# A ring of raw expert weights that keeps its 12 slots to the end, and overflow tables that borrow one of them

## The chip, the core and the metric

The kernel runs on one core of a Trainium2 chip. The metric is the device time of one execution in microseconds (us). The engines that count here are TensorE (PE, matmuls and transposes), VectorE (DVE), ScalarE (ACT), GpSimd (POOL, which also starts the gathers and scatters) and SyncE (SP, which starts the weight loads). Each runs its own list of instructions in order and waits on semaphores for the others.

## The reference

One layer of a hybrid encoder for 1024 tokens of width 1024, in float32. An input projection feeds differential attention and a state-space recurrence; their outputs are projected, added and normalized to h. Then comes the part that the change touches, a mixture of 32 experts: each token goes to the best two experts of the best one of four groups.

```python
for i in range(DEPTH):
    proj = x @ w_in[i]
    ...
    mix = jnp.concatenate([a_out, s_out], axis=-1) @ w_out[i]
    h = _layernorm(alpha * x + mix, ln1_g[i], ln1_b[i])
    moe = _hier_moe(h.reshape(b_ * s_, d_), ...)
    x = _layernorm(alpha * h + moe, ln2_g[i], ln2_b[i])

def block_fn(args):          # 128 rows of one expert
    tok, w, e = args
    xb = h2d[tok]
    hid = jax.nn.silu(xb @ w_gate[e]) * (xb @ w_up[e])
    yb = hid @ w_down[e]
    return yb * w[:, None].astype(yb.dtype)
```

w_gate and w_up are 1024 x 512 per expert, w_down 512 x 1024. An expert that gets more than 128 rows needs further blocks.

## The kernel before

The stages up to the router run until about 590 us and are not touched. Behind them each of the 32 experts is computed for one block of 128 rows. Its weights, 6 MB, come as six chunks of 1 MB: g0 and g1 (the two halves of the gate), u0 and u1 (up), d0 and d1 (down). The chunks are used in the order g0 u0 g1 u1 of expert e, then d0 d1 of expert e - 1; chunk number n counts along that list, so chunk 63 is d1 of expert 9, in short 9d1.

Each chunk passes through two rings. SyncE loads it into a slot of the raw ring (tile rw, `load_next`, loads at L1166 and L1170). Then `split_next` makes two halves of its bits, wh and wl, in one of three places of a second ring: ScalarE casts to wh (L169), VectorE subtracts to get wl (L150). TensorE multiplies both (`product`, L1223 for y, L1232 for g and u): 12 matmuls of 128x512 per chunk, three for each of the four row blocks, 72 per expert.

Around the weights, per expert: GpSimd gathers its 128 rows of h into gx; `tokens` turns them on TensorE into xT (8 transposes, L1196), ScalarE casts xT to xe and VectorE subtracts for the low half; `hidden` takes the activation of g on ScalarE (gx, L1202), multiplies by u on VectorE (L153), turns it on TensorE (hT, 4 transposes, L1206) and splits it into he; `result` scales y on ScalarE (yo, L1239), adds the residual on VectorE (L159), and GpSimd scatters yo to DRAM. xT and y lie in two pairs of PSUM banks: y(e), then xT(e+4), then y(e+2) share one pair.

The raw ring has 12 slots up to chunk 62 (`deep`, NRAW). From chunk NDEEP = 63 on only 6 of them are used (NLESS), and at the product of chunk 75 the other 6 are given back. One of these takes the tables that say which experts have further blocks (`overflow_blocks`, an Area named over), another the constants of the last LayerNorm (lnc, L1331 and L1332).

The order in which the program names the operations is not the order on the engines: a scheduler places each engine's list by its own estimate of durations and by what each instruction has to wait for. So a changed wait can move instructions on every engine. A loop for further blocks follows the experts; with these inputs it runs zero times.

Of the kernel before, what the change touches and what calls it, by code (L numbers as in the profile page):

```python
# [11 lines left out]
F32 = mybir.dt.float32  # L12
F32R = mybir.dt.float32r
BF16 = mybir.dt.bfloat16
# [31 lines left out]
ORDER = (4, 5, 6, 7, 0, 1, 2, 3)    # the tiles of tokens as attention finishes them  # L46
# [3 lines left out]
class Slots:  # L50
    """Eight-KiB pieces of each partition, handed out by the time since they were given back."""
# [29 lines left out]
class Area:  # L81
    """Tiles by name, cut from a few slots; a name that comes again gets the same place."""

    def __init__(self, sl, n, name):
        self.sl, self.tiles = sl, [sl.get([P, 2048], F32, f"{name}{j}") for j in range(n)]
        self.used, self.at, self.turn = [0] * n, {}, {}
# [18 lines left out]
    def close(self):  # L105
        self.sl.put(*self.tiles)
# [3 lines left out]
def tile_kernel(ctx: ExitStack, tc: tile.TileContext, I: dict, out: bass.AP, dbg=None):  # L110
# [15 lines left out]
    def bank(name, which=0):  # L126
        """512 columns: two banks in turn for which = 0, two others for which = 1, or one of these for 2 or 3."""
        if which == 1:
            turn[0] ^= 1
            which = 2 + turn[0]  # L130
        return psum.tile([P, 512], F32, tag=f"bank{which}", name=name, bufs=1 if which else 2)
# [35 lines left out]
    def split(hi, lo, raw, eng=V):  # L167
        """raw = hi + lo, exactly up to twice the bits of a float32r significand."""
        S.copy(hi, raw)  # L169
        sub(lo, raw, hi.bitcast(F32), eng)  # L170
# [12 lines left out]
    def load_w(ct):  # L183
        """A column tile of w_in."""
        r = misc.get("wr", [KT, P])
        SP.dma_start(r, w_in[:, ct * P:(ct + 1) * P].rearrange("(k p) n -> p k n", p=P))
        wraw[ct] = r
# [28 lines left out]
    def proj(ct):  # L216
        """128 columns of x @ w_in, with columns on the partitions: [128, 1024 tokens] in PSUM."""
        first = ct == 12
        if first:
            turn_x(0)  # L220
        wt = split_w(ct)
        o = bank2(f"proj{ct}")

        def products(kt, halves):
            h_, l_ = xh[kt // 2][:, kt % 2, :], xl[kt // 2][:, kt % 2, :]
            for n, (w_, x_) in enumerate(((0, h_), (0, l_), (1, h_))):
                for hs in halves:
                    PE.matmul(o[:, hs], wt[kt // 4][:, w_, kt % 4, :], x_[:, hs],  # L228
                              start=(kt == 0 and n == 0), stop=(kt == KT - 1 and n == 2))

        for halves in ((HALVES[0:1], HALVES[1:2]) if first else (HALVES,)):
            if first and halves == HALVES[1:2]:
                turn_x(1)
                sl.put(*xraw)
            for kt in range(KT):
                products(kt, halves)
        return o

    def proj_u(c4):
        """128 channels of u, laid out as [(7 - step, channel), group, block of 8 steps]."""  # L240
# [37 lines left out]
    def vexp(x, n, name):  # L278
# [19 lines left out]
        # The power of two in two factors, so that each is a normal number.  # L298
# [71 lines left out]
    # a_re and a_im with states on the partitions, twice over.  # L370
# [33 lines left out]
    # Powers 0..8 of lam_bar.  # L404
# [19 lines left out]
    # (lam_bar - 1) / lam  # L424
# [17 lines left out]
    # Unit phases of 8 steps to the powers 1, 2, .., 64; the sine's sign turns in the lower half.  # L442
# [50 lines left out]
    # cos and sin of the phase of block 16 j + l: of l, and of 16 j.  # L493
# [30 lines left out]
    # The working tiles in slots by the order of their last uses.  # L524
# [13 lines left out]
    def ssm_prepare(u):  # L538
        """The matrices of four groups: into the state, within a block of 8 steps, and out of it; and the phases."""
# [16 lines left out]
        # Kernels of lag 0..7, and the Toeplitz matrix over a block's steps.  # L556
# [26 lines left out]
        # Phases of the blocks' starts.  # L583
# [6 lines left out]
    def ssm_unit(u, UT, z2, made):  # L590
        """The recurrence over blocks of 8 steps, y and gelu(y) of four groups."""
        uo = 4 * (u % 2)
        Wm, Tm, M, C, Sn = made
        # What each block adds to the state, turned back by the block's phase.
# [25 lines left out]
        # Twice gelu(y) = y (1 + tanh(sqrt(2/pi) (y + 0.044715 y^3)))  # L620
# [41 lines left out]
    def proj_v(h):  # L662
        """A head's values, with tokens on the partitions."""
# [15 lines left out]
    def proj_k(h):  # L679
        """Per head and part, the rows [high; low] of k."""  # L680
# [37 lines left out]
    def glu(ct, half):  # L718
# [8 lines left out]
        # The sigmoid of a number is a half and half the hyperbolic tangent of its half.  # L727
# [25 lines left out]
    def queries(h):  # L753
        """A head's queries, high and low parts, each on both halves of the partitions."""
# [43 lines left out]
    def weigh(h, i, p_, L, RL, j, po):  # L798
        """p0 / l0 - lam p1 / l1 but for a factor l0, transposed, times the values."""
# [17 lines left out]
    def normalize(h, g, po, RL):  # L817
        """RMS norm over a head's channels, for the four tiles of tokens 4 g .. 4 g + 3."""
# [31 lines left out]
    # Two heads at a time: at first a large tile of one with a small one of the other, then from the last tile down.  # L850
# [63 lines left out]
    def layernorm(t_, w_, o_, gb, quick=False):  # L914
        """o_ = LayerNorm(t_) gb[0] + gb[1], by way of w_. By half rows on one engine where nothing else runs."""
# [31 lines left out]
    iof = cp.tile([P, P], F32, name="iof")      # 0..127 along the row  # L947
    G.iota(iof, pattern=[[1, P]], base=0, channel_multiplier=0, allow_small_or_imprecise_dtypes=True)
    iom = rtile("iom", [NE])                    # 0..31, less 64
    ts(iom, iof[:, 0:NE], 64.0, ALU.subtract)  # L950
    # Of each token's two choices: token - 4096, token + 1024 k - 4096, weight.
# [6 lines left out]
    tri = rtile("tri", [P], BF16)               # 1 where the row is before the column  # L958
# [4 lines left out]
    # LR and LI have had their last readers.  # L963
    flat = [a_.rearrange("p k g -> p (k g)").bitcast(BF16) for a_ in (LR, LI)]
    O = flat[0][:, 0:2 * NT * NE].rearrange("p (k t e) -> p k t e", k=2, t=NT)                 # the chosen experts as rows of 0 and 1
# [3 lines left out]
    rk = cp.tile([P, 2, NT], F32, name="rk")    # rank among the rows of the chosen expert  # L969
    # Of each place in an expert's first block: the token and the row of its result, less 4096 if any, and the weight.  # L970
# [4 lines left out]
    first = cp.tile([P, NE], F32, name="first")     # ALPHA where it is the token's first choice  # L975

    def route(i0, n, eng):
        ti = slice(i0, i0 + n)

        def first_max(v, w, name):  # L980
            """The maximum along the last axis, and its first place as 0 and 1."""
# [35 lines left out]
        # Rows that an expert gets from earlier tokens.  # L1017
# [5 lines left out]
        # The two probabilities, renormalised: 1 / (1 + e) and e / (1 + e), e = exp(second - first).  # L1023
# [80 lines left out]
    w_g, w_u, w_d = I["w_exp_gate"][0], I["w_exp_up"][0], I["w_exp_down"][0]  # L1104
    NRAW, NSPL, NXG = 12, 3, 5
    NDEEP, NLESS = 63, 6
    # The slots of what is needed last hold the chunks after those split first, until these are split.
# [12 lines left out]
    def deep(n):  # L1120
        """The slot of a chunk, and how many chunks may be loaded and not yet split with it."""
        if NSPL <= n < NSPL + NLENT:
            return lent[n - NSPL], NRAW + NLENT
        if n < NDEEP:
            return raw_ring[(n if n < NSPL else n - NLENT) % NRAW], NRAW + (NLENT if n < NRAW + NSPL + NLENT else 0)
        return raw_ring[n % NLESS], NLESS
# [23 lines left out]
    def rows(a, kt):  # L1150
        """The columns of a that meet rows kt % 4 + 4 p of the kt // 4th 512 rows of a weight."""
        return a[:, 512 * (kt // 4) + kt % 4:512 * (kt // 4) + 512:4]
# [4 lines left out]
    def load_next():  # L1157
        n = st_["load"]
        e, m = order[n]
# [31 lines left out]
    def tokens(e):  # L1191
        """The rows of an expert's block, transposed and split."""
# [52 lines left out]
    # Blocks past the first of each expert: how many, whose, and each row's block and place.  # L1245
    def overflow_blocks():
        op = Area(sl, 1, "over")
# [39 lines left out]
        # Those of a first block get block -1.  # L1287
# [10 lines left out]
    for n, (e, m) in enumerate(order):  # L1298
# [19 lines left out]
        if n == NDEEP + NRAW:  # L1318
            spare = raw_ring[NLESS:]
            sl.back(spare)  # L1320
            meta, place, blk = overflow_blocks()
# [6 lines left out]
    sl.back(raw_ring[:NLESS])  # L1328
    # What the last LayerNorm needs besides the experts' results.
# [89 lines left out]
    def moments(i):  # L1419
        """Less the mean, and the variance plus epsilon, of a tile's rows."""  # L1420
# [58 lines left out]
```

## Time and profile before

| | us |
|---|---|
| median of 3 runs | 1226.17 |
| lowest and highest | 1224.1, 1226.75 |
| span of the profiled execution | 1226.3 |
| TensorE busy in it | 1093.3 (89%) |
| VectorE busy | 970.5 (79%) |
| ScalarE busy | 701.1 (57%) |

The profile is of one execution; its span runs from the first to the last instruction and lies within the spread of the three runs, so sums can be made on it. Busy times of an engine are means over stages; the expert stage is read in stretches of its own. A row of a timeline gives the start, the duration and what the instruction writes and reads; buffer numbers are left out, so rw9d stands for both 9d0 and 9d1. In brackets stands the idle time before the instruction and what ended it.

### The profile page before, as it was taken

Reading aid. Unit: us, or ns where it says so; the run is one execution under the profiler, and the core shown is the slowest. Engines: PE = TensorE matmul, PEld = TensorE weight load, DVE = VectorE, ACT = ScalarE, POOL = GpSimd, SP = SyncE. Lnnn points to the kernel's source line nnn. Section 1 sums busy time; section 2 is a strip of 40 time slices with the busy share of each in tenths; the row PEclk is TensorE's granted clock in tenths of the full one; section 3 lists DMA queues with packets and bytes.
Section 4 is the critical chain, followed back from the end, with each engine's and each line's share of the span. In section 5 each row is a group of like instructions: output and inputs, shape, how many; then the busy total and the mean of one; then the engine's idle time right before and its main releaser. Section 6 shows DMA issues by size and latency. Waiting matters only on the chain. (4 is left out here: it accounts for less than half of the span.)

```text
span 1226.3 us, 15046 instructions
## 1 busy us (share of the span) xinstructions
PE 1093.3 (89%) x5313; PEld 902.2 (74%) x5313; DVE 970.5 (79%) x1409; ACT 701.1 (57%) x941; POOL 390.7 (32%) x279
## 2 busy tenths in 40 slices
PE   7987998889899999976999999999999999999910
PEld 6876787767688788875888887877787787777700
DVE  5598678556877664466999998899999989999857
ACT  3222333445675642233788886777778777877702
POOL 0058465322443442343125640213212212121034
PEclk9988999997899899976999999999999999999955
DMA  5641111211201463563899994999999999999666
GB/s 195 148 93 48 42 56 28 57 34 35 68 2 35 141 234 111 208 238 117 312 350 393 374 380 164 358 322 373 361 373 335 366 366 342 394 345 370 239 236 192
DMA packets 89213, 271.01 MB, mean 221 GB/s; under 512 B 30128, under 2 KB 50608, under 8 KB 64688
## 3 DMA queue, kind: packets, MB, share of 16 engines
q1 hardware_dynamic: 65968, 245.18, 54.6%
q0 software_dynamic: 11216, 23.61, 6.6%
q10 hardware_dynamic: 11952, 1.23, 0.7%
q8 instruction: 43, 0.70, 0.2%
q14 instruction: 34, 0.28, 0.1%
HBM read 254.12 MB, written 27.26 MB: 229 GB/s over the span
## 5 line engine op out<-in xcount | busy, mean ns | idle before, releaser
L1138 POOL DMA_INDIRECT moe_dram<-yo,idx x32 | 65.4, 2042 | 337.5 <-DVE yo L159 330.6
L1133 POOL DMA_INDIRECT gx<-h_dram,idx x32 | 82.3, 2570 | 127.9 <-PE g L1232 51.3
L228 PE MATMUL proj<-xh,wa 128*128 128x512 f32 x256 | 76.5, 406 | 1.6 <-ACT ssm L669 1.6
L228 PE MATMUL proj<-xh,wb 128*128 128x512 f32 x256 | 76.0, 409 | 1.6 <-ACT ssm L669 1.6
L1066 PE MATMUL mix<-woh,mx 128*128 128x512 f32 x256 | 73.7, 398 | 0.0
L781 ACT ACTIVATE p<-s,nm 128x1024 f32<-128x1024 f32 (+7 forms) x64 | 47.2, 743 | 26.3 <-DVE nm L794 19.7
L228 PEld LDWEIGHTS proj<-xh,wb 128*128 128x128 f32 x256 | 50.0, 198 | 12.2 <-ACT ssm L669 1.8
L228 PEld LDWEIGHTS proj<-xh,wa 128*128 128x128 f32 x256 | 49.0, 195 | 11.4 <-ACT ssm L669 1.8
L1239 ACT ACTIVATE yo<-y,WT 128x1024 f32<-128x1024 f32 (+1 forms) x33 | 35.9, 1092 | 36.4 <-PE y L1223 36.3
L169 ACT CAST xe<-xT 128x1024 fp32r<-128x1024 f32 x32 | 32.5, 1014 | 40.9 <-PE xT L1196 32.5
L1066 PEld LDWEIGHTS mix<-woh,mx 128*128 128x128 f32 x256 | 47.5, 190 | 9.4 <-DVE mx L150 0.3
L776 PE MATMUL s<-kk,qh 128*128 128x512 f32 (+3 forms) x96 | 42.2, 439 | 11.3 <-ACT p L781 10.4
L159 DVE SCALAR_TENSOR_TENSOR yo<-gx,first,yo 128x1024 f32<-128x1024 f32 (+1 forms) x33 | 41.1, 1249 | 10.3 <-ACT yo L1239 10.1
L1196 PE MATMUL xT<-ident,gx 128*128 128x128 f32 x256 | 37.7, 291 | 9.8 <-DMA gx<-h_dram,idx 9.8
L1196 PEld LDWEIGHTS xT<-ident,gx 128*128 128x128 f32 x256 | 36.9, 207 | 12.6 <-DMA gx<-h_dram,idx 10.4
L150 DVE TENSOR_TENSOR xe<-xT,xe 128x1024 fp32r<-128x1024 f32 x32 | 39.0, 1219 | 8.0 <-ACT xe L169 7.5
L794 DVE TENSOR_REDUCE nm<-s 128x1 f32<-128x1024 f32 (+3 forms) x32 | 32.6, 1020 | 14.6 <-PE s L778 14.6
L814 PE MATMUL po<-vv,half 128*128 128x128 f32 x288 | 42.9, 290 | 0.0
L228 PE MATMUL proj<-xl,wa 128*128 128x512 f32 x128 | 42.8, 404 | 0.0
L228 PE MATMUL proj<-xl,wb 128*128 128x512 f32 x128 | 42.6, 407 | 0.0
L1202 ACT ACTIVATE gx<-g 128x512 f32<-128x512 f32 x32 | 19.1, 596 | 40.3 <-PE g L1232 40.3
L1066 PE MATMUL mix<-wol,mx 128*128 128x512 f32 x128 | 42.1, 397 | 0.0
(862 smaller groups left out, 3547.7 us busy)
## 6 DMA issues: line engine op xcount, KB each, us to landing
misc<-in_w_in_dram SPq DMA_DIRECT2D x16, 512.0 KB, 4.5
mo<-moe_dram SPq DMA_DIRECT2D x11, 512.0 KB, 6.4
xr<-in_x_dram SPq DMA_DIRECT2D x8, 512.0 KB, 5.8
wo_raw<-in_w_out_dram SPq DMA_DIRECT2D x4, 1024.0 KB
xa<-in_x_dram SPq DMA_DIRECT2D x8, 512.0 KB, 4.4
h_dram<-xa SPq DMA_DIRECT2D x8, 512.0 KB, 4.5
out_dram<-mo SPq DMA_DIRECT2D x8, 512.0 KB, 5.9
mo<-moe_dram POOLq DMA_DIRECT2D x5, 512.0 KB, 13.2
```

Source lines behind the costliest of these rows:

```text
L150: eng.tensor_tensor(out=out_, in0=a, in1=b, op=ALU.subtract)
L159: return V.scalar_tensor_tensor(out=out_, in0=a, scalar=s, in1=b, op0=op0, op1=op1)
L228: PE.matmul(o[:, hs], wt[kt // 4][:, w_, kt % 4, :], x_[:, hs], start=(kt == 0 and n == 0), stop=(kt == KT - 1 and n == 2))
L776: PE.matmul(s_[:, c0:c0 + w], qd[0][:, c, tk], kk[h][:, c, c0:c0 + w], start=True, stop=False)
L781: S.activation(p_[:, c, 0:n], s_[:, 0:n], AF.Exp, bias=nm[:, c:c + 1], accum_out=L[:, j, c:c + 1])
L794: V.tensor_reduce(out=nm[:, c:c + 1], in_=s_[:, 0:n], axis=AX.X, op=ALU.max, negate=True)
L814: PE.matmul(po[:, j * P:(j + 1) * P], aT[:, k, :], vv[k // 4][:, k % 4, h * P:(h + 1) * P], start=(k == 0), stop=(k == i))
L1066: PE.matmul(o[-(hs.start > 0)][:, hs], mx[:, m_, kt, :], (woh, wol)[w_][kt // 2][:, kt % 2, hs], start=(kt == 0 and n == 0), stop=(kt == K ...
L1133: G.indirect_dma_start(out=dst, out_offset=None, in_=h_dram[:, :], in_offset=bass.IndirectOffsetOnAxis(ap=ix, axis=0), bounds_check=T - 1, ...
L1138: G.indirect_dma_start(out=moe_dram[:, :], out_offset=bass.IndirectOffsetOnAxis(ap=ix, axis=0), in_=src, in_offset=None, bounds_check=2 * ...
L1196: PE.transpose(b_[:, kt * P:(kt + 1) * P], rows(g_, kt), ident)
L1239: S.mul(yo[:, hs], y[:, hs], WT[:, e:e + 1])
```

## The change

The ring keeps 12 slots for all chunks. The overflow tables are made when chunk 63 (9d1) is about to be loaded, in the slot of the ring that 9d1 then takes; the earlier user of that slot is chunk 51, d1 of expert 7. The load of 9d1 therefore waits for the last operation on the tables. The constants of the last LayerNorm are loaded behind the last weights, when the 12 slots are given back. Comments are removed, which moves lines by 2 or 3 (L1166 becomes L1169, L1202 becomes L1205, L1239 becomes L1242).

```diff
 class Area:
-    def __init__(self, sl, n, name):
-        self.sl, self.tiles = sl, [sl.get([P, 2048], F32, f"{name}{j}") for j in range(n)]
+    def __init__(self, sl, n, name, key=None):
+        self.sl, self.key = sl, key
+        self.tiles = [sl.get([P, 2048], F32, f"{name}{j}") if key is None else sl.at(key, [P, 2048], F32, name)
+                      for j in range(n)]
...
     def close(self):
-        self.sl.put(*self.tiles)
+        if self.key is None:
+            self.sl.put(*self.tiles)
...
-    NDEEP, NLESS = 63, 6
+    NOVER = 63
...
     def deep(n):
         if NSPL <= n < NSPL + NLENT:
             return lent[n - NSPL], NRAW + NLENT
-        if n < NDEEP:
-            return raw_ring[(n if n < NSPL else n - NLENT) % NRAW], NRAW + (NLENT if n < NRAW + NSPL + NLENT else 0)
-        return raw_ring[n % NLESS], NLESS
+        return raw_ring[(n if n < NSPL else n - NLENT) % NRAW], NRAW + (NLENT if n < NRAW + NSPL + NLENT else 0)
...
     def load_next():
         n = st_["load"]
+        if n == NOVER:
+            over.extend(overflow_blocks(deep(n)[0]))
...
-    def overflow_blocks():
-        op = Area(sl, 1, "over")
+    over = []
+    def overflow_blocks(key):
+        op = Area(sl, 1, "over", key)
...
         product(e, m)
-        if n == NDEEP + NRAW:
-            spare = raw_ring[NLESS:]
-            sl.back(spare)
-            meta, place, blk = overflow_blocks()
...
-    sl.back(raw_ring[:NLESS])
+    meta, place, blk = over
+    sl.back([deep(n)[0] for n in range(len(order) - NRAW, len(order))])
     lnc = sl.get([P, 2, D], F32, "lnc")
     SP.dma_start(lnc[:, 0, :], I["ln2_g"][0].partition_broadcast(P))
     SP.dma_start(lnc[:, 1, :], I["ln2_b"][0].partition_broadcast(P))
```

The loads around 9d1 on SyncE before (rw9d1_... is the raw tile of 9d1, and so on):

```order
L1170 DMA rw11g1_5912<-in_w_exp_gate_dram 128x2048
L1170 DMA rw11u1_5933<-in_w_exp_up_dram 128x2048
L1166 DMA rw10d0_5964<-in_w_exp_down_dram 128x2048
L1166 DMA rw9d1_5842<-in_w_exp_down_dram 128x2048
L1170 DMA rw11g0_5863<-in_w_exp_gate_dram 128x2048
L1170 DMA rw11u0_5891<-in_w_exp_up_dram 128x2048
L1331 DMA lnc_9248<-in_ln2_g_dram 128x1024
L1332 DMA lnc_9248<-in_ln2_b_dram 128x1024
L1166 DMA rw10d1_5993<-in_w_exp_down_dram 128x2048
L1170 DMA rw12g0_6014<-in_w_exp_gate_dram 128x2048
```

The same place afterwards:

```order
L1173 DMA rw12g0_5906<-in_w_exp_gate_dram 128x2048
L1173 DMA rw12u0_5934<-in_w_exp_up_dram 128x2048
L1173 DMA rw12g1_5955<-in_w_exp_gate_dram 128x2048
L1173 DMA rw12u1_5976<-in_w_exp_up_dram 128x2048
L1169 DMA rw11d0_6007<-in_w_exp_down_dram 128x2048
L1173 DMA rw13g0_6057<-in_w_exp_gate_dram 128x2048
L1173 DMA rw13u0_6085<-in_w_exp_up_dram 128x2048
L1169 DMA rw9d1_5734<-in_w_exp_down_dram 128x2048
L1340 TENSOR_LOAD meta_5720
L1340 ISA x2
L1173 DMA rw13u1_6127<-in_w_exp_up_dram 128x2048
```

The load of 9d1 has moved behind all loads of expert 12 and behind 13g0 and 13u0, the two lnc loads have left, and a read of meta, the last of the tables, follows 9d1.

ScalarE around the tokens of expert 25 before (yo reads y, xe reads xT, wh casts a chunk, he the hidden rows):

```order
L1239 ACTIVATE yo_4516<-y21_7844,WT_3441 128x1024
L169 CAST wh23u0_7859<-rw23u0_7734 128x1024 x2
L169 CAST wh23g1_7887<-rw23g1_7755 128x1024 x2
L169 CAST wh23u1_7908<-rw23u1_7776 128x1024 x2
L1202 ACTIVATE gx2_4367<-g23_7893 128x512
L169 CAST wh22d0_7929<-rw22d0_7807 128x1024 x2
L169 CAST wh22d1_7960<-rw22d1_7836 128x1024 x2
L169 CAST xe1_4369<-xT25_8098 128x1024
```

ScalarE for experts 25 and 26 afterwards:

```order
L1242 ACTIVATE yo_4516<-y21_7856,WT_3441 128x1024
L172 CAST xe1_4369<-xT25_8110 128x1024
L172 CAST wh25u0_8173<-rw25u0_7897 128x1024 x2
L172 CAST wh25g1_8201<-rw25g1_7918 128x1024 x2
L172 CAST wh25u1_8222<-rw25u1_7939 128x1024 x2
L172 CAST wh24d0_8243<-rw24d0_7970 128x1024 x2
L172 CAST wh24d1_8274<-rw24d1_7999 128x1024 x2
L1205 ACTIVATE gx2_4367<-g25_8207 128x512
L172 CAST wh26g0_8303<-rw26g0_8020 128x1024 x2
L172 CAST he_4514<-hT25_8294 128x512
L1242 ACTIVATE yo_4516<-y22_8007,WT_3441 128x1024
L172 CAST xe0_4368<-xT26_8261 128x1024
```

Before, yo of y21 stands seven rows ahead of the xe that reads xT25. Afterwards it stands directly ahead of it, and he of expert 25 and yo of y22 stand directly ahead of the xe that reads xT26.

## Rows read from the trace of the kernel before

**Rows 1.** Windows of the expert stage; columns in the first row.
```profile
core 0: us, PE busy (x) PEld busy (x) DVE busy (x) ACT busy (x) POOL busy (x), PEclk, DMA share, GB/s
600.00:740.00 140.00, 140.00 (x664) 117.52 (x663) 136.00 (x127) 116.45 (x127) 59.96 (x16) 1.00 0.98 373
740.00:800.00 60.00, 57.24 (x256) 47.10 (x255) 52.18 (x60) 41.73 (x46) 9.57 (x6) 0.94 0.70 259
800.00:1150.00 350.00, 334.97 (x1541) 272.56 (x1540) 322.33 (x308) 270.63 (x297) 68.16 (x35) 1.00 0.96 359
```

**Rows 2.** ScalarE timeline, first gate casts: start us, us, line, operation, count.
```profile
667.44 2.00 ACT L169 CAST wh6g<-rw6g 128x1024 fp32r<-128x1024 f32 x2
...
720.89 2.00 ACT L169 CAST wh9g<-rw9g 128x1024 fp32r<-128x1024 f32 x2
...
801.07 2.01 ACT L169 CAST wh13g<-rw13g 128x1024 fp32r<-128x1024 f32 x2
...
989.84 2.00 ACT L169 CAST wh23g<-rw23g 128x1024 fp32r<-128x1024 f32 x2
...
1103.05 2.00 ACT L169 CAST wh29g<-rw29g 128x1024 fp32r<-128x1024 f32 x2
```

**Rows 3.** TensorE waits (total, times, longest), then ScalarE and VectorE timelines.
```profile
PE u L1232 <- DVE wl20u L150: 0.7, 1, 0.7
...
956.74 1.12 ACT L1239 ACTIVATE yo<-y,WT 128x1024 f32<-128x1024 f32 x1 [1.71 <-PE y L1223]
...
957.89 1.29 DVE L159 SCALAR_TENSOR_TENSOR yo<-gx,first,yo 128x1024 f32<-128x1024 f32 x1 [1.08 <-ACT yo L1239]
959.09 2.36 DVE L150 TENSOR_TENSOR wl21u<-rw21u,wh21u 128x1024 fp32r<-128x1024 f32 x2
```

**Rows 4.** SyncE issue, DMA landing (KB, us) and cast of expert 18's gate.
```profile
880.81 0.33 SPq L1170 DMA_DIRECT2D rw18g<-in_w_exp_gate_dram  x1
...
rw18g<-in_w_exp_gate_dram SPq DMA_DIRECT2D x2, 1024.0 KB, 6.9
...
895.71 2.00 ACT L169 CAST wh18g<-rw18g 128x1024 fp32r<-128x1024 f32 x2
```

**Rows 5.** SyncE: longest wait on its queue, and two issues of loads.
```profile
SPq L1166 <- DVE wl9d L150: 21.3, 1, 21.3
...
730.28 0.33 SPq L1166 DMA_DIRECT2D rw9d<-in_w_exp_down_dram  x1
...
763.16 0.33 SPq L1166 DMA_DIRECT2D rw10d<-in_w_exp_down_dram  x1
```

**Rows 6.** TensorE timeline around 9d1; idle before a row in brackets.
```profile
757.43 1.12 PE L1196 MATMUL xT<-ident,gx 128*128 128x128 f32 x8
760.60 0.73 PE L1223 MATMUL y<-wh9d,he 128*128 128x512 f32 x2 [2.05 <-ACT wh9d L169]
762.05 1.22 PE L1223 MATMUL y<-wl9d,he 128*128 128x512 f32 x2 [0.72 <-DVE wl9d L150]
```

**Rows 7.** TensorE, ScalarE and VectorE timelines of experts 20 and 21.
```profile
963.01 0.39 PE L1232 MATMUL g<-wh21g,xe 128*128 128x512 f32 x1
...
965.73 0.39 PE L1232 MATMUL u<-wh21u,xe 128*128 128x512 f32 x1
...
970.21 1.01 ACT L169 CAST xe<-xT 128x1024 fp32r<-128x1024 f32 x1
...
973.30 0.59 ACT L169 CAST he<-hT 128x512 fp32r<-128x512 f32 x1 [0.19 <-PE hT L1206]
...
969.77 0.68 DVE L153 TENSOR_TENSOR gx<-u,gx 128x512 f32<-128x512 f32 x1
...
972.64 1.22 DVE L150 TENSOR_TENSOR xe<-xT,xe 128x1024 fp32r<-128x1024 f32 x1
```

**Rows 8.** TensorE windows of 2 us: start:end, us, busy (count), clock.
```profile
761.00:763.00 2.00, 1.28 (x4) 0.61 0.00 0
763.00:765.00 2.00, 2.00 (x6) 0.50 0.38 82
765.00:767.00 2.00, 2.00 (x6) 0.50 0.97 406
767.00:769.00 2.00, 2.00 (x8) 0.69 0.99 389
```

## The prediction, before the change was run

> **What bounds the kernel now.** I read the stretches of the expert stage first [rows 1]. Until 740 us TensorE is busy for all of 140 us while the DMA engines are at 0.98: two limits touch. From 740 to 800 it is busy 57.24 of 60 us, at a mean clock of 0.94, and the DMA share falls to 0.70. That is where the ring of raw weights goes from 12 slots to 6. From 800 to 1150 TensorE is busy 334.97 of 350 us. So of the 21 experts behind the change of ring, no stretch is idle for long; what a deeper ring could give back is the difference in rhythm.
>
> The rhythm is read from the first cast of each expert's gate weights on ScalarE [rows 2]. From expert 6 to 9 it is (720.89 - 667.44)/3 = 17.82 us per expert; from 9 to 13, across the change of ring, 80.18 us, which is 8.9 more than four times 17.82; from 13 to 23 it is (989.84 - 801.07)/10 = 18.88; from 23 to 29, 113.21/6 = 18.87. The late rhythm is 1.05 slower than the early one, exactly as long for every expert.
>
> Then I looked at what ends the wait in that rhythm [rows 3]. TensorE waits once per expert, 0.7 us, for the low half of the first up-weights (16 rows of this kind in the list of waits, wl15u to wl30u). VectorE has the raw chunk and its high half, but stands in front of it at yo, the weighted result of the expert before, which itself waits for ScalarE's yo at 956.74. That wait is made by the order in which VectorE and ScalarE take their work, not by a missing chunk. The transfers confirm it [rows 4]: expert 18's first gate chunk is issued at 880.81, such a load takes 6.9 us, so it lies there at about 887.7, and its cast starts at 895.71. Eight us early with 6 slots: the shallow ring isn't late. The order matters, and the change redraws it.
>
> The sum is made on the profiled span, 1226.3 us, which is 0.1 above the median of the runs, 1226.17.
>
> **The change part by part.** No matmul, cast or subtraction of a weight is added or removed. The two dozen small table operations exist before and after, and the comments cost nothing. What changes is which load waits for which slot, and with it the order on all engines.
>
> *Experts 9 to 13.* Before, the load of 10d1 waits 21.3 us on the SyncE queue for the low half of 9d, and is issued at 763.16; 9d1 itself was issued at 730.28 [rows 5]. TensorE then has holes of 2.05 and 0.72 us around 9d1 [rows 6]. Afterwards the tables lie in 9d1's slot, so 9d1's load can't go before the last table operation, a cast that stands on VectorE behind the low half of 11u0; and on SyncE it stands behind the loads of all of expert 12 and of 13u0. 13u0 takes the slot of 11u0, so 9d1 leaves when 11u0 has been split: the last transposes before the hole stand at 757.43 [rows 6], and a cast of 2.0 and a subtraction of 2.4 us later it is about 762. It lands 7 us after that. What covers that is 11g0, 11u0, 11u1 and the first half of y10, 48 matmuls, at 0.227 us each (12 of them between 963.01 and 965.73 [rows 7]) 10.9 us. So the hole moves but is not much larger. The second half of y9, its result, 11g1 and 10d1 then come late together. Bounds: all 8.9 us of today's loss come back; or 9d1 stalls TensorE for the whole 7 us landing plus its 2.0 us cast, +9. I take +2, near today's loss, since one hole is traded for another.
>
> *Experts 13 to 23.* In the new order the casts run d0, g0, xe, d1, gx, u0, u1, yo, g1, he, so yo no longer stands before the first up-weights. The 0.7 us wait [rows 3] goes. Bounds: 0 (yo now stands before the split of g1 and may wait there), and the early rhythm, -1.06 for each of ten experts. I take -0.6, a little under the wait that goes: -6.
>
> *Experts 24 to 27.* Here the new order is worse. Before, ScalarE takes yo of y21 seven rows ahead of the tokens of expert 25, and of y22 seven ahead of 26. Afterwards yo stands directly in front of them: yo of y21 then xe from xT25; he25, yo of y22, xe from xT26. The bank pair of xT25 is that of y21, so the transposes wait for that yo; y23 takes the pair of xT25 and waits until VectorE has read it. On ScalarE he, which needs the last up-matmul of the expert, stands before that yo. So from the last up-matmul of one expert to the first matmul of y, nothing but one hT, one xT and two gate matmuls can run on TensorE. In durations of rows 2, 3, 6 and 7, for 25 to 26: cast of 26g0, whose split slot only comes free at that last matmul, 2.0; he 0.59; yo 1.12; xT 1.12; xe 1.01; the subtraction xe 1.22: 7.1 us, in which TensorE has eight transposes, 1.12, four of hT, half as long, and two matmuls, 0.45: 2.1 of work. So 5.0 idle; with 18.0 of work (72 matmuls at 0.227 are 16.3, twelve transposes 1.7) a period of 23.0, against 18.87: +4.1. From 24 to 25 the casts of 23d1 stand between he and yo as well, 1.9 more: +6. From 26 to 27 xT27 comes before he and yo of y23 is already done: gate cast 2.0, xe 1.01, subtraction 1.22, less 2.1: 2.1 idle, a period of 20.1, +1.2. Together +11. Bounds: if the casts come earlier than I read, the gate cast drops out of all three (-6): +5; if the experts on either side, 23 and 27, run in such a loop too, two more at about +4: +19.
>
> *Experts 27 to 31.* From there the order is again that of the early stretch (g0 u0 yo g1 he u1 d0 d1 gx xe). Four experts by -0.8, between 0 and -1.05: -3.
>
> *The clock.* After the 2.05 us hole TensorE's clock goes from 1.00 to 0.61, 0.50, 0.50 and 0.69 in four slices of 2 us [rows 8], which is the lower of its two levels, 1.2 GHz; the work lost is 0.39 + 0.50 + 0.50 + 0.31 of 2 us, 3.4 us. TensorE had been busy without a hole until then, and in the stretch with 0.7 us waits the clock stays at 1.00 [rows 1]. The holes of 5 to 7 us between experts 24 and 26 are longer than the one that did it, so two more drops, and the 2.1 us hole and the first transition have about an even chance together of one more: 2.5 x 3.4, +9 rounded up. Bounds 0 and +14 (four).
> The Trainium skill, "TensorE: Matmul & The Clock Gate", section "Why this matters for your kernels", tells you to keep the tensor engine free of idle gaps between bursts of matmuls, since it falls back to half rate. This trace agrees: 3.4 us lost behind one hole. It speaks against this change; by the list of rows alone the term is the same.
>
> *The last LayerNorm's constants* are loaded after the last weights instead of at 740.91: 2 DMAs on a queue that has nothing else to do by then, with the experts' last results still to come; 0.
>
> Sum: 2 - 6 + 11 - 3 + 9 = +13: 1239 us.
>
> **The rivals.**
> *Depth was what slowed the late stretch.* The same 0.7 us gap for every expert begins where the ring shrinks, and the early rhythm held with 12 slots. Then all 21 experts run at 17.82 again: 22 x 1.05 and the 8.9 of the transition are 32 us, less what the late load of 9d1 takes back: about 1197. The Trainium skill, "Perfetto Trace Analysis", section "Optimization Strategy", says that the same gap repeating on the engine that should be saturated can mean too little memory for the next tile. It would be this rival. Against it: rows 4, the chunk had landed 8 us before its cast. 4 in 100.
> *The late loop does no harm.* If ScalarE reaches yo and xe while TensorE still has weights split ahead, the loop at 24 to 27 is covered, and only the other terms are left: 2 - 6 - 3 plus one drop, -4 to -7: 1220. For it: VectorE is busy 322.33 and TensorE 334.97 of 350 us [rows 1], so there is some slack to absorb it; against: hT, from which the loop starts, needs the very last up-matmul. 9 in 100.
> *The terms cancel*, a smaller loop (+5) without extra drops of the clock: 1224 to 1229. 5 in 100.
> *The ring doesn't get its depth.* SyncE issues in order, and a 9d1 that waits for the tables holds what is behind it. If TensorE starves there, all of the 7 us landing shows plus a full drop, and the loop's high end adds up: 9 + 19 - 6 - 3 + 14 = +33, 1259. 12 in 100.
>
> **How the numbers follow.** Forecast 70 in 100: 1239, its own range 1229 to 1252. Faster by over 0.2% (2.4 us, about what a measurement of this kernel can tell from no change): 4 + 9 and 1 of the cancelling case, 0.14. Within it: the other 4 of that case and 1 of the forecast's low edge, 0.05. Slower: 0.81. For 8 in 10 the range is 1224 to 1254.
>
> **What would show it.** Right: the casts of expert 25's to 27's gate weights lie 22 to 25 us apart, and TensorE's waits there name xT or xe with 2 to 3 us each; the period from 13 to 23 is 18.0 to 18.5 us and the waits for wl of u0 are gone; the clock falls below 0.7 in two or three stretches instead of one; the load of 9d1 is issued around 760. Wrong: TensorE is over 98% busy from 960 to 1100; or the period from 13 to 23 is as before; or the end is ahead of 1220.

## The result and the profile after: 20 us slower, in the two places named

The changed kernel takes 1245.28 us (median of 4 runs, 1243.16 to 1247.17) against 1225.51 of the kernel before (4 runs, 1224.1 to 1226.75): a ratio of 1.0167 with a 95% interval of 1.0144 to 1.0191, or +19.8 us. The forecast was +13, 1239 us, in a range of 1224 to 1254. The profiled execution took 1243.16, its span is 1241.4.

The windows of the expert stage, as in [rows 1] (us, then busy time of TensorE, its weight loads, VectorE, ScalarE and GpSimd, the granted clock, the DMA share, GB/s):

```profile
600.00:740.00 140.00, 140.00 (x663) 117.30 (x662) 136.27 (x137) 115.24 (x126) 58.97 (x16) 1.00 0.96 364
740.00:800.00 60.00, 50.18 (x201) 38.76 (x200) 45.55 (x53) 35.79 (x40) 11.09 (x5) 0.89 0.79 309
800.00:1150.00 350.00, 333.67 (x1519) 274.26 (x1518) 313.26 (x291) 265.67 (x290) 61.22 (x36) 0.98 0.92 350
```

The stretch up to 740 is as before. From 740 to 800 TensorE loses another 7 us (50.18 busy, before 57.24), at a lower clock. From 800 to 1150 it is busy as long as before, 334 us, but with 22 matmul records fewer and a clock of 0.98: part of that busy time runs at the lower of the two clocks.

The rhythm, as in [rows 2]:

```profile
717.45 2.00 ACT L172 CAST wh9g<-rw9g 128x1024 fp32r<-128x1024 f32 x2
...
801.54 2.00 ACT L172 CAST wh13g<-rw13g 128x1024 fp32r<-128x1024 f32 x2 [0.55 <-PE u L1235]
...
983.64 2.00 ACT L172 CAST wh23g<-rw23g 128x1024 fp32r<-128x1024 f32 x2 [0.94 <-PE u L1235]
...
1119.58 2.00 ACT L172 CAST wh29g<-rw29g 128x1024 fp32r<-128x1024 f32 x2
```

From 9 to 13 it is 84.1 us (before 80.2). From 13 to 23 it is 182.1 us, 18.21 per expert (before 18.88). From 23 to 29 it is 135.9 against 113.2. The middle is faster and the stretches on either side of it are slower.

For a sum I use a mark on TensorE, the start of the first up-matmul of an expert in its timeline, and the end of the last matmul. A mark can shift by 2 us where the order within an expert differs, so only sums over several experts are told. In us:

| kernel | experts 9 to 14 | 14 to 23 | 23 to 28 | 28 to the end | 9 to the end |
|---|---|---|---|---|---|
| before | 101.2 | 170.2 | 94.4 | 77.6 | 443.3 |
| changed | 110.1 | 162.4 | 111.8 | 77.3 | 461.5 |
| difference | +8.9 | -7.8 | +17.4 | -0.3 | +18.3 |

**The first transition.** The timelines of VectorE, SyncE, ScalarE and TensorE (start us, duration us):

```profile
761.32 0.16 DVE L1279 CAST meta<-over 128x16 int32<-128x16 f32 x1
...
761.50 0.33 SPq L1169 DMA_DIRECT2D rw9d<-in_w_exp_down_dram  x1
...
768.37 1.99 ACT L172 CAST wh12u<-rw12u 128x1024 fp32r<-128x1024 f32 x2 [0.26 <-PE y L1226]
770.26 1.99 ACT L172 CAST wh9d<-rw9d 128x1024 fp32r<-128x1024 f32 x2
...
771.36 1.22 PE L1226 MATMUL y<-wh9d,he 128*128 128x512 f32 x2 [3.03 <-ACT wh9d L172]
...
778.85 1.23 PE L1199 MATMUL xT<-ident,gx 128*128 128x128 f32 x8 [1.20 <-ACT yo L1242]
...
781.30 0.60 PE L1235 MATMUL g<-wl11g,xe 128*128 128x512 f32 x1 [0.99 <-DVE wl11g L153]
...
787.49 0.73 PE L1226 MATMUL y<-wh10d,he 128*128 128x512 f32 x2 [1.81 <-ACT wh10d L172]
```

The last table operation, the cast to meta, ends at 761.48, and the load of 9d1 is issued at 761.50; it lands 6.6 us later by the list of transfers, at about 768.1. TensorE has work until 768.33, so the transfer itself is covered. The hole of 3.03 us is a wait for the cast of 9d1, and that cast stands on ScalarE behind the cast of 12u0, which starts at 768.37 and takes 2 us. Then TensorE waits, in one row, for the low half of 9d1 (0.43), for yo (1.20), for the low half of 11g1 (0.99), for 10d1 (1.81) and for an activation (0.71).

**The late loop.** TensorE's waits from 740 to 1180 (total, times, longest):

```profile
PE xT L1199 <- ACT yo L1242: 6.7, 3, 3.8
PE hT L1209 <- DVE gx L156: 4.3, 3, 1.6
PE y L1226 <- ACT wh9d L172: 3.9, 2, 3.0
PE g L1235 <- ACT gx L1205: 2.8, 5, 0.7
...
PE y L1226 <- DVE xe L153: 1.8, 1, 1.8
```

The sixteen waits for the low half of the up-weights [rows 3] are gone. In their place stands xT behind yo. The timelines of ScalarE, VectorE and TensorE around 1050 us, between experts 25 and 26:

```profile
1049.21 1.99 ACT L172 CAST wh26g<-rw26g 128x1024 fp32r<-128x1024 f32 x2
1051.61 0.58 ACT L172 CAST he<-hT 128x512 fp32r<-128x512 f32 x1 [0.40 <-PE hT L1209]
1052.09 1.12 ACT L1242 ACTIVATE yo<-y,WT 128x1024 f32<-128x1024 f32 x1
1054.52 1.01 ACT L172 CAST xe<-xT 128x1024 fp32r<-128x1024 f32 x1 [1.32 <-PE xT L1199]
...
1055.57 1.22 DVE L153 TENSOR_TENSOR xe<-xT,xe 128x1024 fp32r<-128x1024 f32 x1 [0.74 <-ACT xe L172]
...
1027.71 1.98 PE L1199 MATMUL xT<-ident,gx 128*128 128x128 f32 x8 [3.80 <-ACT yo L1242]
...
1050.82 0.75 PE L1209 MATMUL hT<-ident,gx 128*128 128x128 f32 x4 [1.65 <-DVE gx L156]
1053.26 1.23 PE L1199 MATMUL xT<-ident,gx 128*128 128x128 f32 x8 [1.69 <-ACT yo L1242]
1055.59 0.80 PE L1235 MATMUL g<-wh26g,xe 128*128 128x512 f32 x1 [1.10 <-ACT xe L172]
...
1056.85 1.22 PE L1226 MATMUL y<-wh24d,he 128*128 128x512 f32 x2
```

Read it as one chain: hT at 1050.82, he, yo, xT at 1053.26, xe, its low half at 1055.57, and the first matmul of y at 1056.85. Each link waits for the one before; only the first gate matmuls of expert 26 run beside the low half of xe. The cast of 26g0 is no link of it: he waits 0.40 us for hT, not for that cast. The row of 1027.71 is the same place one expert earlier, where the cast of 23d1 stands in the chain too and the wait is 3.80 us.

**The clock.** TensorE in windows of 10 us (us, busy and count, granted clock, DMA share, GB/s):

```profile
770.00:780.00 10.00, 7.01 (x21) 0.66 0.99 412
780.00:790.00 10.00, 6.49 (x18) 0.75 0.45 162
790.00:800.00 10.00, 10.00 (x44) 0.91 0.51 184
...
1020.00:1030.00 10.00, 4.48 (x20) 0.87 0.98 360
1030.00:1040.00 10.00, 9.17 (x33) 0.79 0.40 155
1040.00:1050.00 10.00, 9.18 (x41) 1.00 0.92 356
1050.00:1060.00 10.00, 6.35 (x22) 0.73 0.88 326
1060.00:1070.00 10.00, 10.00 (x42) 0.93 0.35 122
...
1080.00:1090.00 10.00, 9.26 (x34) 0.83 0.80 275
```

The work lost at the lower level, one minus the clock times 10 us, is 6.8 us around 780 and 8.5 us between 1020 and 1090, 15.3 together, in twice as many us at 1.2 GHz. It is an upper bound, since TensorE is idle in a part of them. Before it was 3.4 [rows 8]. In windows of 1 us the clock falls three times in the first stretch, near 771, 781 and 788 us, and in windows of 2 us three times in the second, near 1027, 1055 and 1082.

### The profile page after: what moved, and what is told of

It is laid out like the page before. It is cut to its first block, busy times and chain, and to the rows that moved or that the text cites. A ratio compares the mean times of both kernels' runs of the same rounds, so it can differ in the third digit from the quotient of the medians.

```text
span 1241.4 us, 15031 instructions
## 1 busy us (share of the span) xinstructions
PE 1101.2 (89%) x5313; PEld 909.2 (73%) x5313; DVE 970.2 (78%) x1409; ACT 703.2 (57%) x941; POOL 386.1 (31%) x279
## 3 DMA queue, kind: packets, MB, share of 16 engines
q10 hardware_dynamic: 11952, 1.23, 0.7%
## 5 line engine op out<-in xcount | busy, mean ns | idle before, releaser
L1139 POOL DMA_INDIRECT moe_dram<-yo,idx x32 | 70.1, 2192 | 253.3 <-DVE yo L162 220.8
L1134 POOL DMA_INDIRECT gx<-h_dram,idx x32 | 74.0, 2314 | 233.8 <-issue 74.4
L1242 ACT ACTIVATE yo<-y,WT 128x1024 f32<-128x1024 f32 (+1 forms) x33 | 35.9, 1091 | 21.9 <-PE y L1226 21.9
L817 PEld LDWEIGHTS po<-vv,half 128*128 128x128 f32 x288 | 37.2, 198 | 1.7 <-ACT half L814 0.3
```

The costliest lines, as they stand in the source:

```text
L817: PE.matmul(po[:, j * P:(j + 1) * P], aT[:, k, :], vv[k // 4][:, k % 4, h * P:(h + 1) * P], start=(k == 0), stop=(k == i))
L1134: G.indirect_dma_start(out=dst, out_offset=None, in_=h_dram[:, :], in_offset=bass.IndirectOffsetOnAxis(ap=ix, axis=0), bounds_check=T - 1, ...
L1139: G.indirect_dma_start(out=moe_dram[:, :], out_offset=bass.IndirectOffsetOnAxis(ap=ix, axis=0), in_=src, in_offset=None, bounds_check=2 * ...
L1242: S.mul(yo[:, hs], y[:, hs], WT[:, e:e + 1])
```

## The experiments

The theory is that of the prediction: the ring's depth is worth nothing by itself, and most of the time is lost because the changed waits make the scheduler draw another order, in which yo stands directly ahead of xe. Its rivals: the slot that the tables borrow; weights that come late; and depth as a gain, which an early rhythm would show. Below, "gap 1" counts the experts whose xe stands directly behind the yo of four experts earlier in ScalarE's list; it is none before and two (25, 26) in the changed kernel.

### The borrowed slot without the deep ring

```diff
     def deep(n):
...
-        return raw_ring[(n if n < NSPL else n - NLENT) % NRAW], NRAW + (NLENT if n < NRAW + NSPL + NLENT else 0)
+        if n < NOVER:
+            return raw_ring[(n if n < NSPL else n - NLENT) % NRAW], NRAW + (NLENT if n < NRAW + NSPL + NLENT else 0)
+        return raw_ring[n % 6], 6
...
-    sl.back([deep(n)[0] for n in range(len(order) - NRAW, len(order))])
+    sl.back(raw_ring)
```

> The changed kernel with the ring cut to 6 slots from chunk 63 on, as before; the tables still borrow 9d1's slot and the last constants are still loaded late. Theory (the late loop comes from the order that goes with the deep ring, the borrowed slot costs little): in its order yo stands 6 rows ahead of xe for every expert from 18 on, so no loop; a regular rhythm of 19 us from 14 to 31 and a hole around 9d1 as in the changed kernel: 1226 to 1234 us. Rival (the borrowed slot is the cause): it keeps most of the loss, 1240 or more.

Measured: 1229.76 us (1228.99 to 1231.0), ratio to the kernel before 1.0055 (1.0035 to 1.0075), some 15 us less than the changed kernel. The stretch 9 to 14 is 103.6 us, 14 to 23 168.5, 23 to 28 95.5; gap 1 never occurs. TensorE's waits have the old form again, a little longer, for every expert from 16 on:

```profile
PE u L1237 <- DVE wl16u L153: 0.9, 1, 0.9
```

The borrowed slot and the late constants together are worth a few microseconds; they are not the 20. The load of 9d1 leaves late here too, at 757.30 us, and no wait of TensorE names 9d1. In this order the transition costs +2.4 us from 9 to 14, not +8.9.

### The deep ring without the borrowed slot in the middle

```diff
-    NOVER = 63
+    NOVER = 180
```

> The changed kernel with the tables made at the load of chunk 180 (30g1), so that 9d1 waits for nothing and the ring has 12 slots throughout. Theory (order): in its order yo stands directly ahead of xe for experts 15, 16 and 27, 28, so there are two loops with holes on TensorE of 3 to 7 us per expert instead of one, and two to five more drops of the clock: 1245 to 1270 us, though nothing borrows a slot in the middle. Rival (the borrowed slot and 9d1's late load cost the 20 us): no more than 1226.

Measured: 1261.8 us (1257.59 to 1263.13), ratio 1.0318 (1.0298 to 1.0338). 9d1 waits for nothing, the stretch 9 to 14 is 99.3 us, 1.9 less than before although the loop begins in it, and the kernel is the slowest of all. Gap 1 occurs four times (15, 16, 27, 28), and at the first of these places TensorE's timeline shows the chain of the changed kernel, wait for wait:

```profile
827.36 0.74 PE L1209 MATMUL hT<-ident,gx 128*128 128x128 f32 x4 [1.42 <-DVE gx L156]
...
829.80 1.98 PE L1199 MATMUL xT<-ident,gx 128*128 128x128 f32 x8 [1.69 <-ACT yo L1242]
...
832.88 0.79 PE L1235 MATMUL g<-wh15g,xe 128*128 128x512 f32 x1 [1.10 <-ACT xe L172]
```

1.42, 1.69 and 1.10 us here, 1.65, 1.69 and 1.10 in the changed kernel. The periods are 25.4, 26.7 and 27.1 us in the first loop and 28.0, 27.4 and 27.1 in the second.

### Eleven slots

```diff
-    NDEEP, NLESS = 63, 6
+    NDEEP, NLESS = 63, 11
```

> The kernel before with 11 slots instead of 6 from chunk 63 on; the tables keep their own slot and place. Theory (order): yo stands directly ahead of xe for experts 23 and 24, one loop as in the changed kernel, part of which the faster rhythm elsewhere pays: 1228 to 1246 us. Rival (depth is what the late stretch lacks): the early rhythm of 17.8 us throughout, about 1200.

Measured: 1231.2 us (1230.65 to 1232.93), ratio 1.0069 (1.0049 to 1.0089). This kernel has the early rhythm in places only: 17.8 us per expert from 13 to 18, but 94.5 us from 9 to 14, 18.9 per expert, and 19.0 per expert from 18 to 22. Around 23 and 24, where its gap is 1, the periods are 28.1, 26.6 and 23.4 us and eat up what was won. So a deep ring does come with a faster middle, but whether through the ring or through the order this run doesn't tell.

### The order held by hand, with 12 slots and with 6

Each expert instruction on TensorE, VectorE and ScalarE, and each weight load, is queued behind the one traced before it on its engine, and the expert loop is traced in the order of the early stretch, from expert E0 = 4 on. The tables are made behind the split of chunk 180 (30g1). The run with 6 slots has in addition the same cut of the ring at chunk 63 as the first experiment.

```diff
+    def pin(ins, eng=None):
+        return tc.keep_in_program_order(ins) if pinned[0] and eng is not G else ins
...
+    for e in range(E0, NE + 1):
+        splits(e, "g0")
+        splits(e, "u0")
+        if e > E0:
+            result(e - 2)
+        splits(e, "g1")
+        if e < NE:
+            product(e, "g0")
+        if e > E0:
+            turn_hidden(e - 1)
+        splits(e, "u1")
+        if e < NE:
+            product(e, "u0")
+        splits(e - 1, "d0")
+        if e < NE:
+            product(e, "g1")
+        splits(e - 1, "d1")
+        if e < NE:
+            product(e, "u1")
+            hidden(e)
+        if e + 2 < NE:
+            tokens(e + 2)
+        product(e - 1, "d0")
+        product(e - 1, "d1")
```

> The changed kernel with the order of the weight loads and of all expert work on TensorE, VectorE and ScalarE written out by hand from expert 4 on, in the pattern of the early stretch (g0 u0 yo g1 he u1 d0 d1 gx xe), ring of 12, tables at 30g1. Theory (order): 17.8 us per expert throughout, that is 22 x 1.05 and the 8.9 of the transition less than before, and some 5 us for the tables on VectorE, which is nearly full: 1199 to 1210 us. Rival (a deep ring costs time by itself, by transfers that disturb the gathers or the weights): still 18.8 us or more per expert, 1225 or more.

> The hand-written order of the pinned kernel, word for word, but with the ring cut to 6 slots from chunk 63 on. Theory (depth has no price and no gain of its own, it only changed the order that the scheduler drew): the same 17.8 us per expert and the same time as the pinned kernel with 12 slots within 0.3%, 1201 to 1208 us. Rival (12 slots are what gives the early rhythm): 18.9 us per expert, 1225 us.

Measured: 1204.51 us with 12 slots (1201.38 to 1206.04; ratio 0.9851, 0.983 to 0.9871) and 1203.2 with 6 (1198.49 to 1209.99; ratio 0.9812, 0.9751 to 0.9874). The windows with 12 slots, then those with 6:

```profile
740.00:800.00 60.00, 60.00 (x283) 50.30 (x282) 58.25 (x55) 49.68 (x54) 34.75 (x8) 1.00 0.99 387
800.00:1150.00 350.00, 335.49 (x1557) 279.60 (x1555) 323.53 (x324) 272.35 (x297) 151.54 (x36) 0.98 0.87 334
```

```profile
740.00:800.00 60.00, 60.00 (x285) 50.36 (x284) 57.65 (x55) 49.58 (x54) 29.88 (x7) 1.00 0.89 336
800.00:1150.00 350.00, 344.16 (x1606) 287.51 (x1605) 332.99 (x332) 280.68 (x306) 167.59 (x36) 1.00 0.94 362
```

Both have 60.00 of 60 us in the transition, and by the marks 89.2, 160.5 and 89.2 us for the three stretches, 17.83 us per expert, the same with 6 slots as with 12. (The window from 800 has fewer busy microseconds with 12 slots because that profile reached expert 9 some 11 us sooner and was done with its matmuls at 1141.) Depth is worth nothing in this order. The one hole that is left before the last expert lies where the tables are made, at expert 30:

```profile
1103.39 0.50 PE L1240 MATMUL u<-wl30u,xe 128*128 128x512 f32 x1 [2.70 <-DVE wl30u L158]
```

### The tables in 9d1's slot, with the order held

```diff
-    E0, NOVER = 4, 180
+    E0, NOVER = 4, 63
...
     def load_next():
         n = st_["load"]
+        if n == NOVER:
+            on, pinned[0] = pinned[0], False
+            over.extend(overflow_blocks(deep(n)[0]))
+            pinned[0] = on
...
-            if st_["split"] == NOVER + 1:
-                pinned[0] = False
-                over.extend(overflow_blocks(deep(NOVER)[0]))
-                pinned[0] = True
```

> The pinned kernel with 12 slots, with the tables at the load of 9d1, in 9d1's slot, as in the changed kernel. It prices the borrowed slot and the tables with the order held fast. Theory: the tables cost a hole of about 5 us on TensorE at expert 9, because VectorE is nearly full, and the hole of 3 to 4 us at expert 30 goes, so the total stays: 1201 to 1209 us. Rival (9d1's late load costs the 9 us that the transition lost): a hole of 9 us or more, 1209 to 1216.

Measured: 1204.76 us (1204.29 to 1205.05), ratio 0.9839 (0.9797 to 0.988). The hole sits at expert 9 now, and is the only one of the middle:

```profile
724.11 0.50 PE L1244 MATMUL g<-wl9g,xe 128*128 128x512 f32 x1 [2.47 <-DVE wl9g L158]
```

The period there is 20.6 us, 2.8 over the rule. So the tables and the borrowed slot cost 2.8 us, half of what I expected, with the order held. But 9d1 isn't late here: VectorE makes the tables early, and its load leaves at 725.34 us, where it left at 761.50 in the changed kernel. So this run prices the tables, and a late 9d1 is not tested with the order held.

### The loop by itself

```diff
+    LATE = (24, 25, 26)
...
-        if e > E0:
+        if e > E0 and e not in LATE:
             result(e - 2)
...
-        if e > E0:
+        if e > E0 and e - 1 not in LATE:
             turn_hidden(e - 1)
...
+        if e in LATE:
+            splits(e + 1, "g0")
+            turn_hidden(e)
+            result(e - 2)
         if e + 2 < NE:
             tokens(e + 2)
```

> The pinned kernel with 12 slots, with one thing moved for experts 24, 25 and 26: the cast of the next g0, hT with he, and yo of two experts earlier stand between the last up-matmul and the transposes xT, as the changed kernel has them. Theory: TensorE is idle for 3 to 5 us in each of the three, with one to three drops of the clock of up to 3.4 us: 9 to 20 us more than the pinned kernel, 1214 to 1225. Rival (the loop is harmless, its cover is there): within 3 us of the pinned kernel.

Measured: 1216.21 us (1211.63 to 1217.85, 8 runs), 11.7 above the pinned kernel by the medians; by the marks of the profile, which leave out what differs ahead of expert 9, 7.8 us. The three periods are 20.5 us instead of 17.83. TensorE at the second of them, and its windows of 10 us:

```profile
1027.40 0.74 PE L1215 MATMUL hT<-ident,gx 128*128 128x128 f32 x4 [1.42 <-DVE gx L161]
...
1029.84 0.73 PE L1232 MATMUL y<-wh24d,he 128*128 128x512 f32 x2 [0.73 <-ACT yo L1248]
```

```profile
1000.00:1010.00 10.00, 7.84 (x40) 1.00 0.97 350
1010.00:1020.00 10.00, 10.00 (x46) 1.00 0.96 358
1020.00:1030.00 10.00, 7.85 (x40) 1.00 0.99 388
1030.00:1040.00 10.00, 10.00 (x45) 1.00 0.79 284
```

Two holes of 1.42 and 0.73 us per expert, a cost of 2.7 us each, at a clock that stays at 1.00. The expectation of 3 to 5 us and of a drop of the clock was too high, and 7.8 lies below the 9 to 20 that were forecast; the medians lie within it only by what differs ahead of expert 9. The mechanism costs time, but this is a milder form of it: here y waits for yo, and xT does not. That fits pairs of banks that fell otherwise, which was not read from the runs.

### The changed kernel with its late loop alone taken away

The edit is against the kernel with the tables in 9d1's slot.

```diff
-    E0, NOVER = 4, 63
+    E0, NOVER = 23, 63
```

> The changed kernel, in the scheduler's order up to expert 22, and in the hand-written order from expert 23 on: on TensorE and ScalarE word for word the changed kernel's list up to the first g of expert 23. It takes away the late loop alone; ring of 12, borrowed slot and transition stay. Theory: the 17 us of the loop (experts 23 to 28: 111.8 us of the first up-matmuls against 94.4 before) and the 5 us by which that stretch is slower than five times 17.8 in the kernel before go together: 20 to 25 us less than the changed kernel, 1219 to 1226 us, about the kernel before. Rival (the loop is a symptom, the time is lost to weights that come late): the stretch stays above 100 us, 1235 or more.

Measured: 1224.8 us (1220.37 to 1228.87, 10 runs), 20.5 less than the changed kernel and level with the kernel before (ratio 1.0005, 0.9985 to 1.0024). The stretch 23 to 28 is 91.2 us instead of 111.8, and from 1020 us on TensorE's windows of 20 us there are full, at full clock (18.57 us busy in the one before):

```profile
1020.00:1040.00 20.00, 19.96 (x93) 1.00 0.93 346
1040.00:1060.00 20.00, 20.00 (x95) 1.00 0.97 387
1060.00:1080.00 20.00, 20.00 (x100) 1.00 1.02 419
```

So the order from expert 23 on is worth the 20 us: the 17.4 of the late loop, and some 3 by which the stretch is now faster than before (91.2 against 94.4). The run doesn't part the loop's links. The hand-written order puts yo away from xe, and it also ends the wait of xT for yo and the drops of the clock. In the run before, yo directly ahead of xe without these two cost 7.8 us, against 17.4 for the whole loop; no run has one of the two alone. The ring, the borrowed slot and the transition (107.6 us) are still those of the changed kernel.

### A version that beats both

```diff
-            if st_["split"] == NOVER + 1:
-                pinned[0] = False
-                over.extend(overflow_blocks(deep(NOVER)[0]))
-                pinned[0] = True
...
     result(NE - 1)
     pinned[0] = False
+    over.extend(overflow_blocks(deep(NOVER)[0]))
```

> The pinned kernel with 12 slots and the tables made behind the last expert's result, where VectorE waits for the scatter anyway. Theory: the 2.7 us hole at expert 30 and part of what follows go and nothing is late in the last LayerNorm: 3 to 6 us less than the pinned kernel, 1197 to 1202. Rival (the read of the tables' first number holds up the last loads): 1205 to 1212.

> The fastest kernel so far (pinned order, tables behind the last result) with the ring cut to 6 slots from chunk 63. Theory (depth is worth nothing once the order is held): 17.8 us per expert and the same time within 0.4%, 1196 to 1205 us. Rival (12 slots cover what 6 can't): 1215 or more.

Measured: 1200.69 us with 12 slots (1197.49 to 1204.02; ratio 0.9814, 0.9767 to 0.986) and 1202.25 with 6 (1197.64 to 1202.89; ratio 0.9817, 0.9782 to 0.9853). With the tables behind the last result the hole at expert 30 is gone; from expert 9 to the end it is 417.7 and 418.0 us. That is 22 to 25 us under the kernel before, and again the same with either ring.

## Why the prediction was right, and where its sizes were off

**The transition (+2, and a share of a clock drop).** The step was right: 9d1's load left at 761.50, where about 762 was forecast, and one hole was traded for another. The transfer was covered as the sum had it; of the hole that is left, 2 us are the cast of 12u0 ahead of that of 9d1, an order that the prediction didn't read. The size was off: the transition costs +8.9 us, so +2 was too little. Up to 3.4 of it is work lost to the lower clock beyond that of before (6.8 against 3.4). The rest is what the prediction named ("come late together") and didn't price: behind the hole of 3.03 us there are five more waits, 0.43, 1.20, 0.99, 1.81 and 0.71. With a ring of 6 the load of 9d1 left nearly as late and the transition was only 2.4 us longer than before, which speaks for the order around it as what makes it dear. That is argued: no run has the changed kernel's ring and late load with another order there.

**Experts 13 to 23 (-6).** -6.7 by the casts, -7.8 by the marks from 14. The waits for the low up-weights went, as forecast.

**Experts 24 to 27 (+11) and two clock drops (6.8).** 17.8 were forecast for this stretch and +17.4 measured from 23 to 28. The periods are 27.4, 26.0 and 23.4 us by the marks, 76.8 together with the clock in them; less the 8.5 us at most of work lost to it they are 68.3, where 68.0 was forecast (24.9, 23.0 and 20.1). So the loop had the size of the sum, the clock fell three times instead of twice, and the period of 27, 16.3 us, gives some of it back. In the sum's chain he 0.58, yo 1.12, xT 1.23, xe 1.01 and its low half 1.22 stand as forecast in the rows of 1050 us. Its first link, the cast of 26g0 with 2.0 us, was another one there: that cast runs beside VectorE's product and hT, which take 2.4 us from the end of the last up-matmul to the end of hT. That these two are about equally long was luck. The casts of the gates of 25, 26 and 27 lie 26.9 and 26.0 us apart, more than the 22 to 25 named as a sign.

**Experts 27 to 31 (-3).** Nearly nothing can be read here, -0.3, since the marks shift where the order changes and 23 to 28 holds part of it. From the casts of 28 to 31 it is 53.3 against 58.3 us, but the last expert starts earlier against its matmuls.

**The clock (+9).** 15.3 us of work lost against 3.4: +11.9, all of it already counted in the transition and the late loop above. There were six drops against one before, three at the first transition and one each at experts 25, 26 and 27, so five more where 2.5 were forecast; they were shorter than the 3.4 us of the sum, 2.6 on average. The price of a drop and their number were both off, in opposite directions.

**The sum.** It was made on the span of 1226.3 us and not on the time of a run. A run's time is some 1.8 us above its span (1243.16 and 1241.4 in the changed kernel), so by that the span of before would belong to an execution about 2 us slower than the median. Against +19.8 this is small. By the marks the parts add up to +18.3; the terms that came out low, the transition above all and the stretch from 27 on, are why +13 was too little.

**The rivals.** That depth would restore the early rhythm (4 in 100) is refuted with the order held: 6 slots have it as well. The Trainium skill, "Perfetto Trace Analysis", section "Optimization Strategy", says that the same gap repeating can mean too little memory for the next tile; in this case the measurement decides against that reading, 17.83 us per expert with 6 slots and with 12. That the late loop does no harm is refuted by taking it away. That the terms cancel is refuted by the result. The bound that 9d1 stalls TensorE for its whole landing came out in size, +9 forecast and +8.9 measured, but not in kind: the landing was covered.

What stays open is why the scheduler places yo later with a deep ring. The three kernels with 11 or 12 slots in its own order have a gap of 1 somewhere and the two with 6 slots have none; what in its estimate makes the difference wasn't tried. Open too is how the loop's 17.4 us divide between the order on ScalarE, the wait of xT for yo and the clock.

## What to carry to other kernels

Before more buffers are added, look at when a buffer's content lands and when it is used: 8 us between the two [rows 4] said that depth was worth nothing, and a repeated gap of 0.7 us was made by two engines' order. Where a scheduler draws the order, a change of one wait redraws all of it, so read the new order for an instruction that now stands directly ahead of one that depends on it across three engines. Holding the order of a good stretch by hand gave 19 to 22 us, about what the change took, and 22 to 25 with the tables at the end.

## What the runs showed of the hardware that was not expected

The clock falls behind some holes and not behind others, and the length of a hole alone does not sort them. These are the waits for the tables at expert 30 in the pinned kernel with 6 slots and in the run of the loop by itself:

```profile
1114.29 0.51 PE L1242 MATMUL u<-wl30u,xe 128*128 128x512 f32 x1 [2.56 <-DVE wl30u L158]
...
1120.63 0.50 PE L1241 MATMUL u<-wl30u,xe 128*128 128x512 f32 x1 [2.55 <-DVE wl30u L158]
```

Behind the first the granted clock stays at 1.00 up to 1130 us; behind the second it is 0.50 from 1122 to 1124. It also stayed at 1.00 through three periods with holes of 1.42 and 0.73 us and behind the single hole of 2.47 us at expert 9. It fell behind 2.05 and 0.72 us in the kernel before, behind 2.70 us in the pinned kernel with 12 slots, around the hole of 3.80 us, and around 1.65, 1.69 and 1.10 us in one row.

The executions differ ahead of the change. In the twelve profiles, one of each kernel, the first up-matmul of expert 2 starts between 594.9 and 606.1 us. TensorE waits for the first two gathers of rows in all of them, 5.46 to 6.22 us and 1.16 to 3.56 us. Most of the difference is older: the first gather starts between 550.07 and 558.39 us. Where it comes from was not read. That is why parts are compared from expert 9 on.
